# A neighbourhood-attention encoder layer: 23 key columns in the first block, values and gates requested earlier, raw attention-half weights split during attention

## The chip, the cores and the metric

The kernel runs on one core of one Trainium2 chip. Its time is the device time of one execution in microseconds, and the figure that is compared is the median of several executions. The profile is one more execution, recorded by the hardware profiler.

## The reference

One encoder layer is applied to a prompt (256 tokens, a grid of 4 rows) and to a sample (2048 tokens, 32 rows of 64 columns), all in float32. Half of the mixed width is neighbourhood attention, the other half a Fourier mixer.

```python
def neighbourhood_attention(q, k, v, rpb):          # window of 8 rows x 16 columns
    def one_row(r):
        rs = jnp.clip(r - kr // 2, 0, rows - kr)
        k_slab = lax.dynamic_slice_in_dim(kg, rs, kr, axis=1)[:, :, slab_cols]   # 32 columns per block of 16
        v_slab = lax.dynamic_slice_in_dim(vg, rs, kr, axis=1)[:, :, slab_cols]
        logits = jnp.einsum('bjqhd,bijkhd->bhjqik', q_blk, k_slab) * scale
        logits = jnp.where(valid[:, :, None, :], logits + bias, NEG_INF)
        p = softmax(logits)
        return jnp.einsum('bhjqik,bijkhd->bjqhd', p, v_slab)

def encoder_layer(x, ...):
    h = rms_norm(x, g_pre)
    q, k, v, z_a, u_f, z_f = jnp.split(h @ w_in, ...)          # six parts of 512
    y_a = neighbourhood_attention(q, k, v, rpb)                # 8 heads of 64
    y_f = fourier_mix(u_f, w_fourier, b_fourier)
    mixed = jnp.concatenate([rms_norm(y_a, g_na) * silu(z_a), rms_norm(y_f, g_f) * silu(z_f)], -1)
    return x + rms_norm(mixed @ w_out, g_post)
```

A query column of the first block (columns 0 to 15) sees key columns 0 to 22 at most, one of the last block (48 to 63) key columns 40 to 63.

## The kernel before

Each float32 product of the projections is three matmuls on a high and a low part (`mm3`). The program has four stretches: projections up to about 550 us, the Fourier mixer up to about 612, attention up to about 860, and the output's last product. The order of the instructions on each engine is the order of the code (`manual_schedule`); every DMA goes out on SP's queue except one or two at the start on ACT's, and each transfer waits on one of eight semaphores in turn, so for the landing of the one eight before it.

The projections use their own weights and, between them, prepare `w_out`: `wo_load` fetches a raw block of 128 x 1024, `wo_split` makes the high and low part on ACT and DVE (scaled by `gmix`) and stores both in `woD`. There are eight blocks: 0 to 3 belong to the attention half, 4 to 7 to the Fourier half.

Attention is 36 groups in four rounds, one round for each pair of heads (`pr`), nine groups in a round (`i`): the prompt, then row blocks `R` = 0 to 3 in two column halves `hc`. A group holds 256 queries in two blocks of columns (`b`); `KW` gives the key columns that are kept for the four blocks, 24, 32, 32, 24. A group of `R` > 0 has 11 key rows in reach, a group of `R` = 0 has 8. One step `k` of the loop works on two groups at once: for the new group `g` = G[k] the score matmuls (tile `s`), bias and minimum on DVE (`bias_max`), the exponentials on ACT (`exps`), the scaling on POOL (`soft`); for the group before it, `f` = G[k-1], the transposes of the weights (`transp`, tile `ptb`), their copies (`pt`) and the product with the values (`pv`). Between them PE does half a tile of the Fourier half's output product (`f_mm`, tile `po`), which `f_evac` scales and stores in `oD`. Its operands come by `ys_load`, `ys_mul` (gate `yz`, on POOL) and `ys_split`.

At the end of step `k`, `prep_v` requests the values and gate `za` of G[k+1] (three buffers, `VB`) and `prep` the queries of G[k+3]. The values lie in `vD`, one array of rows for each block of columns. With 24 columns, four key rows fill 96 partitions, and 11 rows make three chunks of 96, 96 and 72; `ch` lists the chunks that are transposed and `pp` the pv matmuls. `load_t` and `mask_p` bring and mask the bias tables of the next round: the table is requested in step i = 5 and masked in step i = 8. From step 24 to 31 the split weights of the attention half come back from `woD`, 512 KB a step.

After the last attention step come 18 tiles of output (`a_mm`, `evac`, `factor`, `residual`). `last_tile` is the last of them; it also finishes the tile before it, `b`.

Of the kernel before, what the change touches and what calls it, by code (L numbers as in the profile page):

```python
# [31 lines left out]
KW = (24, 32, 32, 24)  # L32
# [9 lines left out]
VB = 3  # L42
# [3 lines left out]
def constants():  # L46
# [62 lines left out]
    for p in range(128):  # L109
        half, i, qc = p // 64, p // 16 % 4, p % 16  # L110
        for b in range(2):
            cb = 2 * b + half
            ws = min(max(16 * cb + qc - 8, 0), 48)
            kc = KP0[cb] + np.arange(32)
            cm[p, b] = np.where((kc >= ws) & (kc < ws + 16), 0.0, BIG)
        for cb, j in ((0, slice(0, 24)), (1, slice(24, 56)), (3, slice(56, 80))):
# [62 lines left out]
def build(tc, A, O):  # L179
# [20 lines left out]
    woD = dr.tile([2, 2, 4, 128, D], F32, name="woD")  # L200
# [169 lines left out]
    VC = ((0, 0, 0, 24, 0), (1, 0, 8, 24, 0), (1, 1, 0, 8, 24), (2, 0, 24, 8, 0), (2, 1, 0, 24, 8), (3, 1, 8, 24, 0))  # L370
# [253 lines left out]
    def x_part(c, kp, q=nc.sync):  # L624
        if kp == 0:
            xs[c] = gt(BS, F32, "xr")
        ks = slice(2 * kp, 2 * kp + 2)
        q.dma_start(xs[c][:, ks], xsrc(c)[:, ks])
# [72 lines left out]
    def wo_load(x):  # L701
        wor[x] = load((128, D), A["wo"][x // 4, x % 4], "wr")

    def wo_split(x):
        w = wor.pop(x)
        g = gmix[:, x:x + 1]
        o = k8(F32R, "wo", (128, 2, D))
        nc.scalar.activation(o[:, 0], w, AF.Copy, scale=g)
        nc.vector.scalar_tensor_tensor(out=o[:, 1], in0=w, scalar=g, in1=f_(o[:, 0]), op0=ALU.mult, op1=ALU.subtract)
        for y in range(2):  # L710
            nc.sync.dma_start(woD[x // 4, y, x % 4], f_(o[:, y]))
# [118 lines left out]
    for i in range(16):  # L830
        sg, pr = divmod(i, 8)
        if i == 8:
            hooks.clear()
            for x in (5, 6):
                at(2 * x - 9, b_split, x)
            for x in range(8):
                if x:
                    at(3 * x - 2, wo_load, x)
                at(3 * x + 2, wo_split, x)
            at(20, w_load, 8)  # L840
            at(24, w_sums, 8)
            for j in range(7):
                at(24 + j // 2, a_split, 8, j)
            vu(1, range(4), hooks)
# [271 lines left out]
    def prep_v(g):  # L1116
# [99 lines left out]
    for n in range(2):  # L1216
        for c in range(4):
            nc.sync.dma_start(wo1[n][c].bitcast(F32),
                              woD[1, :, c, :, n * 512:n * 512 + 512].rearrange("x p d -> p x d"))
# [159 lines left out]
    def ys_load(d):  # L1379
# [141 lines left out]

    NT = {4: range(2, 4), 8: range(4, 8), 10: range(8, 13), 12: range(13, 18)}
# [19 lines left out]
    ys_load(ftiles[2])  # L1542
    prep_v(G[2])
    prep(G[4])
    for k in range(2, len(G) + 1):
# [11 lines left out]
        if k == 23:  # L1557
# [34 lines left out]
        if g:  # L1592
            soft(g, 1)
            if k == 2:
                ys_mul(ftiles[x])
                ys_load(ftiles[x + 1])
# [8 lines left out]
        if pr < 3 and i == 8:  # L1605
# [11 lines left out]
        if k + 1 < len(G):  # L1617
            prep_v(G[k + 1])
# [38 lines left out]

    def factor(d, q=1):
        sa, r = d["sa"], d["r"]
        s, y, x = r[:, 0:1], r[:, 1:2], r[:, 2:3]  # L1660
        V.tensor_scalar(s, sa[:, q:q + 1], -0.5 / D, sa[:, 4:5], ALU.mult, ALU.add)
# [3 lines left out]
    def residual(d, n):  # L1665
        of, xt, s = d["of"], d["xt"], d["r"][:, 0:1]
        ns = slice(n * 512, n * 512 + 512)
        if "og" in d:
            V.scalar_tensor_tensor(out=xt[:, ns], in0=d["og"][:, ns], scalar=s, in1=xt[:, ns], op0=ALU.mult,
                                   op1=ALU.add)  # L1670
        else:
            V.scalar_tensor_tensor(out=of[:, ns], in0=ptb[n], scalar=s, in1=of[:, ns], op0=ALU.mult, op1=ALU.mult)
            nc.gpsimd.tensor_tensor(out=xt[:, ns], in0=of[:, ns], in1=xt[:, ns], op=ALU.add)
# [3 lines left out]
    def last_tile(d, b):  # L1677
# [17 lines left out]
        V.tensor_tensor(out=og[:, 512:], in0=ptb[1], in1=d["of"][:, 512:], op=ALU.mult)  # L1695
        factor(d, 3)
        for n in range(2):
            residual(d, n)
# [49 lines left out]
```

## Time and profile before

| | |
|---|---|
| median of the runs | 959.66 us (958.94 to 960.04, 3 runs) |
| the profiled execution | 962.69 us |
| its span, first to last instruction | 960.9 us |
| PE, weight loads | 947.7, 792.8 us busy |
| DVE, ACT, POOL | 666.7, 468.3, 342.1 us busy |
| DMA | 270.64 MB, 282 GB/s in the mean |
| granted TensorE clock, mean | 0.996 |

In the rows of a profile, PE is the matmul engine and PEld its weight loads, DVE, ACT and POOL are the vector, scalar and general engines, SP issues DMAs. `L1484` is a line of the kernel, `pv<-pt,v` says that the instruction writes tile `pv` and reads `pt` and `v`, and `x32` counts instructions. A row of the timeline or of the chain starts with its start and its length in us. A row of the waits names who waited, for whom, for how long in total, how often, and the longest.

### The profile page before, as it was taken

The page shows a single profiled execution, that of the slowest core. Times are in us where ns is not written, and L with a number is a line of the kernel's source. Part 1 is how long each engine was busy: PE and PEld are TensorE (multiplying, and loading weights), DVE is VectorE, ACT ScalarE, POOL GpSimd, SP SyncE. Part 2 cuts the span into 40 slices and gives each one's busy share as a digit, 9 for nine tenths or more (in the row PEclk, how much of TensorE's full clock was granted, in tenths as well). Part 3 has the DMA queues.
Part 4 walks back from the last instruction along what each step waited for, and adds up shares of the span by engine and source line. Part 5 has one row for each costly group of instructions (what it writes and reads, how often), then busy time and mean ns, then how long its engine had stood idle before and what let it go on. Part 6 is the DMA issues. An engine that isn't in the chain of part 4 may idle for free.

```text
span 960.9 us, 17852 instructions
## 1 busy us (share of the span) xinstructions
PE 947.7 (99%) x6240; PEld 792.8 (83%) x6240; DVE 666.7 (69%) x1303; ACT 468.3 (49%) x1035; POOL 342.1 (36%) x338
## 2 busy tenths in 40 slices
PE   8999999999999999999999999999999998999996
PEld 7889988888888888888888888888887886888885
DVE  6387988676866976786667354676656655559997
ACT  6745676522332632233444144666555655544443
POOL 3101202445750401534433000554456555424444
PEclk9999999999999999999999999999999999999999
DMA  9899686458666999479989788599888899899993
GB/s 343 313 356 365 216 291 249 164 229 287 249 232 238 355 414 328 185 258 330 323 277 327 265 304 314 207 252 269 279 266 258 258 284 281 259 307 332 346 339 118
DMA packets 158361, 270.64 MB, mean 282 GB/s; under 512 B 22656, under 2 KB 98304, under 8 KB 155392
## 3 DMA queue, kind: packets, MB, share of 16 engines
q1 hardware_dynamic: 157984, 269.37, 81.4%
q8 instruction: 50, 0.82, 0.3%
q14 instruction: 39, 0.32, 0.1%
q10 hardware_dynamic: 288, 0.14, 0.1%
HBM read 180.91 MB, written 95.88 MB: 288 GB/s over the span
## 4 chain that ended last, share of the span: by engine, by line
PE 95%; DMA 2%; DVE 1%; issue 1%; SPq 0%; ACT 0%; DVEq 0%; ACTq 0%
PE po L1413 19%; PE mm L175 18%; PE mm L176 18%; PE mm L174 18%; PE pv L1484 5%; PE ptb L1467 4%; PE s L1169 4%; PE pab L1014 2%; DMA v<-vD 1%; PE py L174 1%; PE py L176 1%; PE py L175 1%; DMA q<-qD 1%; DMA xr<-xt 0%; PE ppq L1051 0%
## 5 line engine op out<-in xcount | busy, mean ns | idle before, releaser
L174 PE MATMUL mm<-xh,wa 128*128 128x512 f32 x448 | 174.4, 389 | 0.0
L175 PE MATMUL mm<-xl,wa 128*128 128x512 f32 x448 | 174.3, 389 | 0.0
L176 PE MATMUL mm<-xh,wa 128*128 128x512 f32 x448 | 174.3, 389 | 0.0
L1203 POOL TENSOR_SCALAR w<-w,m 128x352 f32<-128x352 f32 (+4 forms) x136 | 77.3, 583 | 61.8 <-DVE m L1200 54.0
L176 PEld LDWEIGHTS mm<-xh,wa 128*128 128x128 f32 x448 | 84.1, 188 | 17.6
L174 PEld LDWEIGHTS mm<-xh,wa 128*128 128x128 f32 x448 | 84.1, 188 | 17.4
L175 PEld LDWEIGHTS mm<-xl,wa 128*128 128x128 f32 x448 | 84.1, 188 | 17.4
L1413 PE MATMUL po<-wo,yh 128*128 128x512 f32 x272 | 90.4, 413 | 0.0
L551 POOL TENSOR_TENSOR ws<-wr 128x512 f32<-128x512 f32 x16 | 22.4, 1397 | 185.9 <-DMA wr<-wz 105.2
L1413 PE MATMUL po<-w,yh 128*128 128x512 f32 x280 | 86.7, 391 | 0.0
L566 DVE TENSOR_TENSOR wa<-wr,wa 128x512 fp32r<-128x512 f32 x60 | 55.0, 924 | 34.7 <-ACT wa L565 34.6
L1196 ACT ACTIVATE w<-w,m 128x352 f32<-128x352 f32 (+4 forms) x136 | 70.2, 519 | 13.3 <-DVE m L1191 13.1
L175 PE MATMUL mm<-vl,xh 128*128 128x512 f32 x168 | 65.5, 390 | 0.2 <-DVE vl L497 0.2
L174 PE MATMUL mm<-vh,xh 128*128 128x512 f32 x168 | 65.4, 389 | 0.0
L176 PE MATMUL mm<-vh,xl 128*128 128x512 f32 x168 | 65.4, 389 | 0.0
L868 DVE TENSOR_TENSOR f<-u,mm 128x512 f32<-128x512 f32 x64 | 43.5, 680 | 30.4 <-PE mm L176 25.8
L1413 PEld LDWEIGHTS po<-w,yh 128*128 128x128 f32 x280 | 52.3, 188 | 10.8
L1191 DVE CUSTOM_DVE_ANT_1 w<-s,tb 128x264 f32<-128x264 f32 (+3 forms) x124 | 51.6, 453 | 11.4 <-PE s L1169 10.9
L1484 PEld LDWEIGHTS pv<-pt,v 96*64 96x64 f32 (+2 forms) x1088 | 45.1, 137 | 15.1 <-issue 11.7
L565 ACT CAST wa<-wr 128x512 fp32r<-128x512 f32 x60 | 36.3, 618 | 41.6 <-PE mm L176 17.7
L1413 PE MATMUL po<-w,yl 128*128 128x512 f32 x140 | 54.5, 389 | 0.0
L1413 PE MATMUL po<-wo,yl 128*128 128x512 f32 x136 | 53.5, 393 | 0.0
(245 smaller groups left out, 2212.3 us busy)
## 6 DMA issues: line engine op xcount, KB each, us to landing
wr<-wz SPq DMA_DIRECT2D x48, 512.0 KB
vl<-sD SPq DMA_DIRECT2D x20, 512.0 KB
xm<-xm SPq DMA_DIRECT2D x9, 1024.0 KB
oD<-ofs SPq DMA_DIRECT2D x18, 512.0 KB
of<-oD SPq DMA_DIRECT2D x18, 512.0 KB
yr<-yD SPq DMA_DIRECT2D x34, 256.0 KB
zD<-f SPq DMA_DIRECT2D x16, 512.0 KB
woD<-wo SPq DMA_DIRECT2D x16, 512.0 KB
```

The costliest lines, as they stand in the source:

```text
L174: nc.tensor.matmul(out, lh, rh, start=first, stop=False)
L175: nc.tensor.matmul(out, lh, rl, start=False, stop=False)
L176: nc.tensor.matmul(out, ll, rh, start=False, stop=last)
L566: nc.vector.tensor_tensor(out=o[:, 1], in0=src, in1=o[:, 0].bitcast(F32), op=ALU.subtract)
L868: nc.vector.tensor_tensor(out=dst(f, b), in0=src(uu[u]), in1=src(p), op=op)
L1169: nc.tensor.matmul(sp[2 * b + h][64 * y:64 * y + 64, j * w:(j + n) * w], g["q"][hs, 128 * b + 64 * y:128 * b + 64 * y + 64], kk[hs, k:k + ...
L1191: nc.vector.tensor_tensor_reduce(out=rows(g["w"][b][:, h, :n], w), in0=rows(g["s"][2 * b + h][:, :n], w), in1=tv, scale=1.0, scalar=3.0e38 ...
L1196: nc.scalar.activation(w, w, AF.Exp, bias=m[:, h:h + 1], scale=-1.0, accum_out=m[:, 2 + h:3 + h])
L1203: nc.gpsimd.tensor_scalar(w, w, m[:, 4 + h:5 + h], 1.0, ALU.mult, ALU.mult)
L1413: nc.tensor.matmul(p, (d["l"] if x == 2 else d["h"])[:, c], w(n, int(x == 1), c), start=j == 0, stop=j == 11)
L1467: nc.tensor.transpose(ptb[h][:nk, j * 128:j * 128 + 128], g["w"][b][:, h, c0:c0 + nk], ident)
L1484: nc.tensor.matmul(p[hs, b, o], g["v"][:nk, v, hs], g["pt"][b][:nk, h, j * 128 + o.start:j * 128 + o.stop], start=first, stop=last)
```

## The change

The first block keeps 23 key columns. Eleven rows are then 253 keys, which make two chunks, of 128 and 125, cut without regard to rows; the values of such a group come in three requests (256 rows as two blocks of 128, then 92 and 36 rows), and its four partial-window products use a third block that holds the rows shared by both halves of queries in the order that the first chunk has. `VB` becomes 4, and values and gates are requested for G[k+2]; Fourier tiles and their gates one tile earlier, `yz` in two buffers. The table of the next round is masked in step i = 7. Only the Fourier half of `w_out` is split in the projections; the raw attention half is fetched in eight parts of 128 x 512 in every second step from 13 to 27 and split in the even steps from 18 to 32. At the start `x_part(0, 0)` goes out on SP's queue. In `last_tile` the rest of tile `b` and the half mean move, and the last sums are cut into two parts of 384 on DVE and one of 256 on ACT and POOL.

```diff
-KW = (24, 32, 32, 24)
+KW = (23, 32, 32, 24)
...
-VB = 3
+VB = 4
...
+    nc.scalar.dma_start(gpre, A["gpre"])
     nc.sync.dma_start(RV[0][:, 0], A["wv"][0][:, 0])
-    nc.scalar.dma_start(gpre, A["gpre"])
-    x_part(0, 0, nc.scalar)
+    x_part(0, 0)
...
-            for x in range(8):
+            for x in range(4):
                 if x:
-                    at(3 * x - 2, wo_load, x)
-                at(3 * x + 2, wo_split, x)
+                    at(6 * x - 2, wo_load, x)
+                at(6 * x + 2, wo_split, x)
...
+            if g["R"] and 11 * w <= 256:
+                vs = src.rearrange("r c e -> (r c) e")[:, cs]
+                k0, k1, m = (r0 - 4) * w, (r1 + 3) * w, 11 * w - 128
+                nc.sync.dma_start(v[:, 4 * b:4 * b + 2], vs[k0:k0 + 256].rearrange("(j p) e -> p j e", p=128))
+                nc.sync.dma_start(v[:n, 4 * b + 2], vs[k1:k1 + n])
+                nc.sync.dma_start(v[n:, 4 * b + 2], vs[k0 + n:k0 + 128])
+                g["ch"].append([(0, 128), (128, m)])
+                g["pp"].append([(1, None, m, 4 * b + 1, True, False), (0, 0, 128, 4 * b, False, False),
+                                (0, 1, 128, 4 * b + 2, False, True)])
+                continue
...
-            d["z"] = sm.tile([128, 4, 128], F32, tag="yz", name="yz", bufs=1)
+            d["z"] = sm.tile([128, 4, 128], F32, tag="yz", name="yz", bufs=2)
...
+    def wo_split_a(y):
+        c, ns = wo_part(y)
+        h, l, w = WO[0][:, c, ns], WO[1][:, c, ns], wraw[:, y % 4 * 512:y % 4 * 512 + 512]
+        nc.scalar.activation(h, w, AF.Copy, scale=gmix[:, c:c + 1])
+        V.scalar_tensor_tensor(out=l, in0=w, scalar=gmix[:, c:c + 1], in1=h.bitcast(F32), op0=ALU.mult,
+                               op1=ALU.subtract)
...
-        if 24 <= k < 32:
-            y = k - 24
-            nc.sync.dma_start(WO[y % 2][:, y // 2].bitcast(F32), woD[0, y % 2, y // 2])
+        if 13 <= k < 29 and k % 2:
+            y = (k - 13) // 2
+            c, ns = wo_part(y)
+            nc.sync.dma_start(wraw[:, y % 4 * 512:y % 4 * 512 + 512], A["wo"][0, c][:, ns])
...
-                if x + 1 < 18:
-                    ys_load(ftiles[x + 1])
+                if x + 2 < 18:
+                    ys_load(ftiles[x + 2])
...
+        if 18 <= k < 34 and k % 2 == 0:
+            wo_split_a((k - 18) // 2)
...
-        if pr < 3 and i == 8:
+        if pr < 3 and i == 7:
             mask_p(pr + 1)
...
-        if k + 1 < len(G):
-            prep_v(G[k + 1])
+        if k + 2 < len(G):
+            prep_v(G[k + 2])
...
-        residual(b, 1)
         sa = d["sa"]
         V.tensor_scalar(sa[:, 0:1], sa[:, 0:1], sa[:, 1:2], None, ALU.add)
         part_sum(sa)
+        residual(b, 1)
         guess(d, 3)
+        half_mean(d, 3)
         V.tensor_tensor(out=og[:, 512:], in0=ptb[1], in1=d["of"][:, 512:], op=ALU.mult)
         factor(d, 3)
-        for n in range(2):
-            residual(d, n)
+        xt, f = d["xt"], d["r"][:, 0:1]
+        nc.scalar.activation(og[:, 768:], og[:, 768:], AF.Copy, scale=f)
+        nc.gpsimd.tensor_tensor(out=xt[:, 768:], in0=og[:, 768:], in1=xt[:, 768:], op=ALU.add)
+        for q, ns in ((nc.sync, slice(0, 384)), (nc.sync, slice(384, 768)), (nc.scalar, slice(768, 1024))):
+            if ns.stop < D:
+                V.scalar_tensor_tensor(out=xt[:, ns], in0=og[:, ns], scalar=f, in1=xt[:, ns], op0=ALU.mult, op1=ALU.add)
+            q.dma_start(O["yo"][d["t"] * 128:d["t"] * 128 + 128, ns], xt[:, ns])
```

On PE, in the step in which the last group of column half 0 of round 0 is transposed and multiplied with its values, the kernel before has these rows (a row is line, operation, out<-in, shape, count; `ptb` is a transpose, `pv` a product with values):

```order
L1467 MATMUL ptb<-ident,w 96x128 x2
L1467 MATMUL ptb<-ident,w 72x128
L1467 MATMUL ptb<-ident,w 96x128 x2
L1467 MATMUL ptb<-ident,w 72x128
...
L1484 MATMUL pv<-pt,v 64x128 x4
L1484 MATMUL pv<-pt,v 64x64 x4
L1484 MATMUL pv<-pt,v 64x128 x4
L1484 MATMUL pv<-pt,v 64x64 x4
```

and the changed kernel these:

```order
L1477 MATMUL ptb<-ident,w 128x128
L1477 MATMUL ptb<-ident,w 125x128
L1477 MATMUL ptb<-ident,w 128x128
L1477 MATMUL ptb<-ident,w 125x128
...
L1494 MATMUL pv<-pt,v 64x128 x2
L1494 MATMUL pv<-pt,v 64x64 x4
L1494 MATMUL pv<-pt,v 64x128 x4
L1494 MATMUL pv<-pt,v 64x64 x4
```

Block 0 has four transposes for six and two wide products for four; block 1 is as it was.

On SP, around the turn to the last round (steps 26 to 28), the kernel before requests the values of the first group of the sample (`vD_64`, `vD_65`) behind the table `tb`, a block of split weights `w` and two stores:

```order
L1085 DMA tb<-tD 128x2x880
L1562 DMA w_7838<-woD 128x1024
L1443 DMA oD<-ofs 128x1024
L1518 DMA yD<-y 128x512
L1134 DMA v<-vD_64 96x2x128 x2
L1134 DMA v<-vD_65 128x2x128 x2
L1146 DMA za<-zD 128x128 x2
L1113 DMA q<-qD 128x2x128
L1562 DMA w_7837<-woD 128x1024
```

In the changed kernel the same values stand ahead of the table, and behind it come a raw part `wraw` and the values of the group after:

```order
L1144 DMA v<-vD_64 92x2x128 x2
L1144 DMA v<-vD_65 128x2x128 x2
L1156 DMA za<-zD 128x128 x2
L1113 DMA q<-qD 128x2x64 x2
L1085 DMA tb<-tD 128x2x880
L1586 DMA wraw<-wo 128x512
L1453 DMA oD<-ofs 128x1024
L1528 DMA yD<-y 128x512
L1144 DMA v<-vD_66 128x2x128 x2
L1144 DMA v<-vD_67 96x2x128 x2
```

The values are one step further up; the queries (`q`) keep their step.

On DVE, at the end of the program, from the last evacuation on, before:

```order
L1638 SCALAR_TENSOR_TENSOR of<-pl,inva,of 128x128
L1672 SCALAR_TENSOR_TENSOR of<-ptb,sr,of 128x512
L1692 TENSOR_SCALAR sa<-sa 128x1
L1649 TENSOR_SCALAR sa<-sa 128x1
L1650 TENSOR_SCALAR sa<-sa 128x1
L1695 TENSOR_TENSOR og<-ptb,of 128x512
L1661 TENSOR_SCALAR sr<-sa 128x1
L1662 TENSOR_SCALAR sr<-sr 128x1
L1663 TENSOR_SCALAR sr<-sr 128x1
L1669 SCALAR_TENSOR_TENSOR xt<-og,sr,xt 128x512 x2
```

and after:

```order
L1664 SCALAR_TENSOR_TENSOR of<-pl,inva,of 128x128
L1717 TENSOR_SCALAR sa<-sa 128x1
L1675 TENSOR_SCALAR sa<-sa 128x1
L1676 TENSOR_SCALAR sa<-sa 128x1
L1698 SCALAR_TENSOR_TENSOR of<-ptb,sr,of 128x512
L1685 TENSOR_SCALAR sr<-sa 128x1
L1722 TENSOR_TENSOR og<-ptb,of 128x512
L1692 TENSOR_SCALAR sr<-sr 128x1
L1693 TENSOR_SCALAR sr<-sr 128x1
L1729 SCALAR_TENSOR_TENSOR xt<-og,sr,xt 128x384 x2
```

The product of the other tile (`of<-ptb,sr,of`) has moved from ahead of the three sums to behind them, and the half mean (L1661, now L1685) from behind `og` to ahead of it.

More of the change, by code (lines that the diff above doesn't have):

```diff
@@ L115, in constants @@
             cm[p, b] = np.where((kc >= ws) & (kc < ws + 16), 0.0, BIG)
-        for cb, j in ((0, slice(0, 24)), (1, slice(24, 56)), (3, slice(56, 80))):
+        for cb, j in ((0, slice(0, 23)), (1, slice(24, 56)), (3, slice(56, 80))):
             ws = min(max(16 * cb + qc - 8, 0), 48)
@@ L199, in build @@
     yD = dr.tile([2, 4, 128, T], F32, name="yD")
-    woD = dr.tile([2, 2, 4, 128, D], F32, name="woD")
+    woD = dr.tile([2, 4, 128, D], F32, name="woD")
     tD = dr.tile([4, 128, 2, 1520], F32, name="tD")
@@ L701, in wo_load @@
     def wo_load(x):
-        wor[x] = load((128, D), A["wo"][x // 4, x % 4], "wr")
+        wor[x] = load((128, D), A["wo"][1, x], "wr")
     def wo_split(x):
         w = wor.pop(x)
-        g = gmix[:, x:x + 1]
+        g = gmix[:, 4 + x:5 + x]
         o = k8(F32R, "wo", (128, 2, D))
@@ L710, in wo_split @@
         for y in range(2):
-            nc.sync.dma_start(woD[x // 4, y, x % 4], f_(o[:, y]))
+            nc.sync.dma_start(woD[y, x], f_(o[:, y]))
     wor = {}
@@ L1218, in build @@
             nc.sync.dma_start(wo1[n][c].bitcast(F32),
-                              woD[1, :, c, :, n * 512:n * 512 + 512].rearrange("x p d -> p x d"))
+                              woD[:, c, :, n * 512:n * 512 + 512].rearrange("x p d -> p x d"))
     prep(G[2])
@@ L1542, in build @@
     ys_load(ftiles[2])
+    ys_load(ftiles[3])
     prep_v(G[2])
     prep(G[4])
+    prep_v(G[3])
     for k in range(2, len(G) + 1):
@@ L1667, in residual @@
         ns = slice(n * 512, n * 512 + 512)
[L1668 to L1673, printed above, removed]
+        V.scalar_tensor_tensor(out=of[:, ns], in0=ptb[n], scalar=s, in1=of[:, ns], op0=ALU.mult, op1=ALU.mult)
+        nc.gpsimd.tensor_tensor(out=xt[:, ns], in0=of[:, ns], in1=xt[:, ns], op=ALU.add)
         nc.sync.dma_start(O["yo"][d["t"] * 128:d["t"] * 128 + 128, ns], xt[:, ns])
```

20 lines of the change are left out of this document (13 added, 7 removed).

## The prediction

> **What bounds the kernel now.** I read the page's first lines, then the tensor engine's waits, the busy time in stretches of 20 us, and last the chain of waits and the timeline at the places where the tensor engine (PE) stands still.
>
> ```profile
> span 960.9 us, 17852 instructions
> PE 947.7 (99%) x6240; PEld 792.8 (83%) x6240; DVE 666.7 (69%) x1303; ACT 468.3 (49%) x1035; POOL 342.1 (36%) x338
> ...
> PE pv L1484 <- DMA v<-vD: 1.9, 2, 1.7
> PE mm L174 <- DVE xh L295: 1.3, 1, 1.3
> PE s L1169 <- DMA q<-qD: 1.2, 3, 0.5
> ...
> 0.00:20.00 20.00, 17.58 (x69) 14.36 (x70) 12.19 (x25) 12.18 (x27) 5.36 (x9) 0.91 0.90 330
> 480.00:500.00 20.00, 20.00 (x90) 16.57 (x89) 13.92 (x18) 9.00 (x15) 7.90 (x6) 1.00 0.76 265
> 700.00:720.00 20.00, 20.00 (x228) 16.41 (x226) 12.41 (x42) 11.42 (x35) 11.28 (x17) 1.00 0.86 256
> 800.00:820.00 20.00, 16.97 (x208) 13.46 (x210) 9.52 (x32) 9.66 (x29) 9.12 (x16) 1.00 0.91 263
> 940.00:960.00 20.00, 13.49 (x69) 11.63 (x67) 15.09 (x36) 6.64 (x21) 8.94 (x7) 0.91 0.32 118
> ```
>
> Behind the length of each stretch stand PE, PEld, DVE, ACT and POOL busy, then PE's granted clock, the DMA engines' share and GB/s. PE idles 13.2 us in all: 2.4 in the first stretch, 3.0 at 800 to 820, 7.4 at the end, some 0.3 elsewhere. So time comes from fewer PE instructions, or from those three places; what is taken off another engine at 480 or 700 is worth nothing by itself.
>
> **The narrower keys.** Only the groups of column block 0 in row blocks R = 1 to 3 lose PE work: 3 in each of 4 head pairs, 12 in all. Each loses two of its twelve transposes and two of its sixteen pv matmuls, those 128 wide. The price is read from the length of an attention step, from the first score matmul to the next:
>
> ```profile
> 744.62 1.21 PE s L1169 x20
> 749.63 1.08 PE pv L1484 x32
> 750.71 1.21 PE s L1169 x20
> 756.14 1.50 PE pv L1484 x32
> 757.64 1.21 PE s L1169 x20
> 758.85 0.81 PE ptb L1467 x6
> ```
>
> A step takes 750.71 - 744.62 = 6.09 us when the group before had 8 transposes and 32 pv records 64 wide (two records to a matmul), and 757.64 - 750.71 = 6.93 with 12 transposes and half the records 128 wide. Of the 0.84 between, pv is 1.50 - 1.08 = 0.42; the other 0.42 is four transposes, 0.105 each. A narrow record is 1.08 / 32 = 0.034, a wide one (1.50 - 16 x 0.034) / 16 = 0.060. So a group loses 2 x 0.105 + 4 x 0.060 = 0.45 us; scores fall by 22 of 1232 columns of 1.21 us, 0.02. Twelve groups give 5.6, the four of R = 0 (184 columns for 192) 0.1 more: **-5.7 us**. Ends: 4.2 (wide records priced as narrow ones), 6.7 (0.81 / 6 a transpose). All of it is on PE's path, as no engine is near 20 of 20 at 700 to 720; DVE, ACT and POOL lose a little with it.
>
> **v and gates earlier, and no split weights fetched.** The last round (pr = 3) stalls:
>
> ```profile
> 733.94 0.92 PE s L1169 x16
> 771.49 1.21 PE s L1169 x20
> 791.67 0.92 PE s L1169 x16
> 794.23 8.58 DMA v<-vD
> 804.87 5.58 DMA v<-vD
> 814.21 5.09 DMA q<-qD
> 822.95 1.23 PE pna L1457 x12
> 835.15 1.21 PE s L1169 x20
> ...
> woD<-wo SPq DMA_DIRECT2D x16, 512.0 KB
> ...
> w<-woD SPq DMA_DIRECT2D x8, 512.0 KB
> tb<-tD SPq DMA_DIRECT2D x4, 880.0 KB
> ```
>
> From step 19 to step 25 round 2 takes 771.49 - 733.94 = 37.55 us; the same steps of round 3, 28 to 34, take 835.15 - 791.67 = 43.48, less 1.23 of pna matmuls that only they have, 42.25. So the stall is 4.7 us, of which the waits show 3.0; the rest hides in score matmuls that run slowly. Its cause stands beside it: v of step 28's group is issued on SP at 794.23, 2.6 after its step began, and lands 8.6 later, behind an 880 KB table, 512 KB of split weights and the store of oD. Round 2 moves 256 GB/s at a share of 0.86, so some 298 fill the engines; 512 KB in each step of about 6.5 us is 81 more, 337, too much.
>
> After the change v goes out a step earlier (6.9 us, where 2.6 of lateness made the first stall), ahead of that table, and the weights are eight loads of 256 KB in every second step from 13 to 27, half the bytes, none from step 28 on. q is not requested earlier; its 1.2 us of waits go only because SP is less late. I take all **-4.7** for the profiled execution; the lower end is 1 (q's waits stay and v gains little).
>
> The third request per group: SP issues 12 more transfers, some 0.45 us each by the issue at 1.17 below, on a queue that in round 2 makes PE wait nowhere. Cover: the step that v now has in hand; uncovered 12 x 0.45 = 5.4 us. The gates' second buffer and the tile loaded two ahead keep SP's wait for the POOL product of the same tile: 0, hidden the same way; v, za and oD queue behind that wait as before. Table masking one step sooner: one POOL instruction, three times, behind a load two steps old; POOL has 7.5 of 20 free. 0; a late table would hold up POOL's scaling and then the transposes, and only then cost.
>
> **The split in attention.** Eight times a 128x512 ACT scaling and a DVE subtraction, at the even steps 18 to 32, after both transposes' copies:
>
> ```profile
> 8.78 0.72 ACT L264 ACTIVATE wc<-rv,gpre 128x512 fp32r<-128x512 f32 x1
> 9.62 0.75 DVE L265 SCALAR_TENSOR_TENSOR wc<-rv,gpre,wc 128x512 fp32r<-128x512 f32 x1
> ```
>
> 0.75 us in every second step, where DVE idles 7.6 of 20 and ACT 8.6: 0. Behind it on DVE stand f_evac and pv's product, whose banks PE needs a step later. Uncovered: 8 x 0.75 = 6 us. What leaves the projections (four splits, eight stores) leaves a stretch with PE at 20.00 of 20: 0.
>
> **The start.** x's first part moves from ACT's queue to SP's, behind the first 256 KB of wv.
>
> ```profile
> 1.17 0.45 ACTq L628 DMA_DIRECT2D xr<-xt  x1
> 4.73 1.49 ACT L264 ACTIVATE wc<-rv,gpre 128x512 fp32r<-128x512 f32 x2 [1.59 <-DMA gpre<-gpre]
> 5.69 0.29 DVE L295 CAST xh<-xr 128x256 fp32r<-128x256 f32 x1 [4.79 <-DMA xr<-xt]
> 6.13 0.47 PE L174 MATMUL mm<-wc,xh 128*128 128x512 f32 x1 [1.33 <-DVE xh L295]
> ```
>
> PE's first product waits for x alone; its other operand is there at 4.73 + 0.75 = 5.48. An earlier x gains at most about 0.5; SP's later loads go out one issue, 0.45, later, so the loss is at most that. **-0.2**, since x no longer shares the engines with what SP queued after it.
>
> **The tail.** After the last matmul the chain runs on ACT and DVE.
>
> ```profile
> 952.40 0.61 DVE L1638 SCALAR_TENSOR_TENSOR of<-pl,inva,of 128x384 f32<-128x384 f32 x1
> 953.79 0.74 DVE L1672 SCALAR_TENSOR_TENSOR of<-ptb,sr,of 128x512 f32<-128x512 f32 x1
> 954.88 0.15 DVE L1650 TENSOR_SCALAR sa<-sa 128x1 f32<-128x1 f32 x1
> 954.95 0.68 DVE L1695 TENSOR_TENSOR og<-ptb,of 128x512 f32<-128x512 f32 x1
> 955.54 0.21 DVE L1661 TENSOR_SCALAR sr<-sa 128x1 f32<-128x1 f32 x1
> 956.17 0.21 DVE L1663 TENSOR_SCALAR sr<-sr 128x1 f32<-128x1 f32 x1
> 956.47 1.42 DVE L1669 SCALAR_TENSOR_TENSOR xt<-og,sr,xt 128x512 f32<-128x512 f32 x2
> ```
>
> The other tile's 0.74 at 953.79 was free, inside ACT's squares; now it stands ahead of og: +0.74. The half mean moves ahead of og and leaves the chain: -0.3. The last adds are two of 0.61 in place of two of 0.71, with 256 columns on ACT and POOL beside them: -0.2; the last transfer is smaller: -0.05. **+0.2**, ends -0.3 and +0.7.
>
> **Sum.** The profiled execution took 962.69 (span 960.9 and 1.8 around it): 962.69 - 5.7 - 4.7 - 0.2 + 0.2 = 952.3. The median of the runs is 959.66, 3.0 less, and since PE's busy time is the same work, that must come out of its idle places. If all of it is stall that the timed runs don't have, only 4.7 - 3.0 = 1.7 is left to win there: 959.66 - 5.7 - 1.7 = 952.3. If none, 959.66 - 10.4 = 949.3. No row says which, so I take the middle, **950.8**.
>
> **Rivals.** (a) The stall stays: SP remains late through the extra issues, q is as late as before, and only PE's work falls: 959.66 - 5.7 = 954.0, up to 956.5 if 2.5 of new stall comes with it. For it: q's waits. Against it: 3.5 MB less in the last round (2 x 256 KB for 8 x 512). (b) Slower: the DMA queue becomes the bound in rounds 1 and 2 as well, since the transfers of 92 and 36 rows and the raw weights come on top of a share of 0.86. Two more rounds with the stall of the last, 4.7 each, while the last keeps its own: 959.66 - 5.7 + 9.4 = 963.4. It decides from the point where a step's added transfer time passes 0.14 x 6.7 = 0.9 us; the raw weights are 256 KB in 13.4 us, 20 GB/s or 0.07, so the narrow transfers would have to bring another 0.07, and eat the step that v has gained. (c) The split holds up PE: 950.8 + 6 = 956.8 with no cover at all; DVE's free 7.6 of 20 speaks against it.
>
> The Trainium skill (DMA: Bandwidth & Descriptors, "Why a DMA increments its semaphore by 16 and not by 1") speaks against this change: a transfer runs on the largest number of engines up to 16 that divides its outer dimension. By it 96 rows use 16 engines, but 92 only 4 and 36 twelve. Estimated by that page, the four engines get 18 more rows of 512 bytes for a group of R > 0 and 68 for R = 0, at 27 ns a row (298 GB/s over 16) 3.4 us in a round of 58, which with the raw weights stays just under the idle 0.14; by it (a) and (b) grow and the sum would go to some 954. No row of this trace has such a transfer.
>
> **How the numbers follow.** The forecast, with the stall gone for the most part (947.5 to 953): 0.62; (a) 953 to 957: 0.22; (b) 0.07; (c) and smaller mishaps of its kind, 956 to 959: 0.06; better than 947.5: 0.03. The range 947.5 to 956.5 leaves out (b), most of (c), and the last. About 0.2% is what this measurement can tell from no change, 957.7 to 961.6: faster 0.87 (the forecast, (a), better), same 0.06 (c), slower 0.07 (b).
>
> **What would show it.** Right: pv of the twelve groups at about 1.26 us and their first transposes x4; PE busy near 942; no PE wait on v or q after 780, 820 to 840 at 20.00; first product near 5.9; some 7.6 us behind the last matmul. Wrong: waits on v or q in steps 13 to 30 with the DMA share above 0.95, PE waiting on pt or w copies at even steps, or matmuls that take longer with 125 and 128 rows.

## The result, and the profile after

The changed kernel took 965.63 us in the median (962.40 to 968.11, 6 runs), the kernel before 959.66 (958.94 to 960.43, 6 runs on the same chip): a ratio of 1.0062, interval 1.0043 to 1.0081. It is slower by 6 us (0.6%), where 950.8 was forecast, and outside the range (947.5 to 956.5). The profiled execution took 968.11, the longest of the six, and its span is 966.3; the one before took 962.69.

The page's first lines, the tensor engine's waits, and the busy time in stretches (PE, PEld, DVE, ACT, POOL, then granted clock, DMA share, GB/s), after:

```profile
span 966.3 us, 17710 instructions
PE 944.9 (98%) x6168; PEld 788.5 (82%) x6168; DVE 669.8 (69%) x1307; ACT 469.6 (49%) x1040; POOL 349.2 (36%) x339
...
PE s L1179 <- DMA q<-qD: 11.9, 8, 2.9
...
700.00:720.00 20.00, 19.03 (x197) 15.04 (x190) 11.29 (x41) 11.19 (x35) 11.00 (x17) 1.00 0.84 253
720.00:740.00 20.00, 18.04 (x208) 14.69 (x204) 11.26 (x43) 10.92 (x37) 10.14 (x17) 1.00 0.87 266
780.00:800.00 20.00, 17.11 (x204) 13.91 (x203) 10.39 (x41) 10.44 (x33) 11.24 (x16) 1.00 0.87 249
800.00:820.00 20.00, 17.08 (x174) 13.16 (x176) 9.97 (x35) 9.46 (x31) 10.14 (x17) 0.83 0.89 264
```

The kernel before had, in two of the same stretches:

```profile
720.00:740.00 20.00, 20.00 (x237) 15.97 (x233) 11.79 (x47) 11.73 (x38) 10.94 (x18) 1.00 0.85 252
780.00:800.00 20.00, 20.00 (x206) 15.95 (x205) 12.05 (x52) 12.18 (x45) 12.51 (x21) 1.00 0.97 303
```

PE has 72 matmuls fewer, and the waits for v are gone. In their place stands one row: the score matmuls wait for q, eight times, 11.9 us, where it was 1.2. The stretches at 700, 720 and 780, in which PE was busy for 20 of 20 us before, now have 1 to 3 us of idle time each. The one at 800 keeps its 3 us and now also runs at a granted clock of 0.83. Why q is late stands in the chain of waits (start, length, what; pieces of 0.14 us and less left out), here at the step in which PE stands still for 2.9 us:

```profile
773.65 8.10 DMA oD<-ofs
781.77 2.68 DMA q<-qD
784.59 1.28 PE s L1179 x20
...
799.68 6.92 DMA oD<-ofs
806.62 4.32 DMA q<-qD
```

and in SP's rows of the timeline (start, length of the issue), with what SP waited for from 779 to 782 under them:

```profile
772.93 0.60 SPq L1586 DMA_DIRECT2D wraw<-wo  x1
773.65 0.35 SPq L1453 DMA_DIRECT2D oD<-ofs  x1
774.11 0.38 SPq L1528 DMA_DIRECT2D yD<-y  x1
774.58 0.88 SPq L1135 DMA_DIRECT2D v<-vD  x1
775.51 1.81 SPq L1136 DMA_DIRECT2D v<-vD  x1
777.37 0.50 SPq L1137 DMA_DIRECT2D v<-vD  x1
777.92 1.38 SPq L1144 DMA_DIRECT2D v<-vD  x2
779.62 0.33 SPq L1156 DMA_DIRECT2D za<-zD  x1
781.77 0.37 SPq L1113 DMA_DIRECT2D q<-qD  x1
...
SPq L1113 <- DMA oD<-ofs: 1.8, 1, 1.8
```

Count from the 512 KB store of `oD`: it, `yD`, three narrow requests, two of the other block, `za` are eight. q is the one after these, so it needs the semaphore of the store, which lands 8.10 us after its issue. SP has nothing to do from 779.95 to 781.77, the DMA engines are not full (0.87 in the mean of 780 to 800), and PE waits. With two requests instead of three q would have stood one place further forward, and would have waited for the landing of the request before the store instead. With eight requests in flight at most, eight go out in the landing time of a slow one, and a step of 6.5 us holds nine to ten (SP issues 58 from 650 to 690).

This block is 1.82 of the 2.90 us for which PE waits. In the second stall SP stands still for 0.91 us before the q at 806.62, of 2.92. The rest is that q comes last behind requests that are issued one after the other, each for 0.33 to 1.81 us in the rows above. In the second stall no third request stands between the store and q: `yD`, four requests of `v` and two of `za` do. So the third request is not alone in making q late.

What SP waited for in round 1 (668 to 728) shows how the queue has filled. The first rows for before, then after (who waited, for whom, total, times, longest):

```profile
SPq L1443 <- ACT ofs L1442: 3.8, 2, 2.1
SPq L1518 <- DVE y L1504: 2.2, 2, 1.3
```

```profile
SPq L1156 <- DMA yr<-yD: 1.0, 2, 0.5
SPq L1113 <- DMA oD<-ofs: 0.8, 1, 0.8
SPq L1528 <- DVE m L1210: 0.8, 2, 0.4
```

Before, SP waited for engines to finish what it was to store: it was abreast of them. After, no wait for an engine is above 0.8: SP is mostly behind, and a request's place in its queue then decides when it goes out.

The stall also costs clock. The last rows of the chain are another q behind another store; for it PE is idle from 808.16 to 811.08. In finer stretches, the first of them behind the 2.9 us at 781.69:

```profile
785.00:788.00 3.00, 3.00 (x35) 2.45 (x28) 2.18 (x10) 1.84 (x7) 0.00 (x0) 1.00 1.13 295
...
808.00:810.00 2.00, 0.16 (x6) 0.02 (x2) 0.42 (x1) 0.39 (x1) 0.15 (x1) 1.00 0.44 103
810.00:811.00 1.00, 0.00 (x0) 0.00 (x0) 0.00 (x0) 0.00 (x0) 1.00 (x2) 0.52 0.87 252
...
812.00:814.00 2.00, 2.00 (x19) 1.35 (x12) 1.23 (x6) 0.60 (x2) 0.00 (x0) 0.50 0.84 245
...
816.00:818.00 2.00, 2.00 (x11) 1.54 (x10) 0.49 (x2) 0.81 (x4) 0.51 (x2) 0.78 0.95 296
```

After this idle time PE works at half clock from 811 to about 817, which is some 3 us more: this stall counts twice. While PE stands still from 808 to 810, the DMA engines are busy for a share of 0.44 only.

### The profile page after: what moved, and what is told of

Same layout as the page of the kernel before. It is cut to its first block, busy times and chain, and to the rows that moved or that the text cites. A ratio compares the mean times of both kernels' runs of the same rounds, so it can differ in the third digit from the quotient of the medians.

```text
span 966.3 us, 17710 instructions
## 1 busy us (share of the span) xinstructions
PE 944.9 (98%) x6168; PEld 788.5 (82%) x6168; DVE 669.8 (69%) x1307; ACT 469.6 (49%) x1040; POOL 349.2 (36%) x339
## 4 chain that ended last, share of the span: by engine, by line
PE 87%; DMA 8%; SPq 2%; DVE 1%; issue 1%; POOL 0%; ACT 0%; POOLq 0%; DVEq 0%; ACTq 0%
PE mm L175 18%; PE mm L176 18%; PE mm L174 18%; PE po L1423 16%; DMA oD<-ofs 3%; PE ptb L1477 3%; PE s L1179 3%; PE pv L1494 3%; PE pab L1014 2%; DMA q<-qD 2%; DMA yz<-zD 1%; DMA v<-vD 1%; PE py L174 1%; PE py L176 1%; PE py L175 1%
## 5 line engine op out<-in xcount | busy, mean ns | idle before, releaser
L1213 POOL TENSOR_SCALAR w<-w,m 128x352 f32<-128x352 f32 (+6 forms) x136 | 81.5, 613 | 79.1 <-DVE m L1210 65.5
L1206 ACT ACTIVATE w<-w,m 128x352 f32<-128x352 f32 (+6 forms) x136 | 70.3, 521 | 25.9 <-DVE m L1201 25.8
L566 DVE TENSOR_TENSOR wa<-wr,wa 128x512 fp32r<-128x512 f32 x60 | 57.8, 972 | 33.6 <-ACT wa L565 33.6
L1201 DVE CUSTOM_DVE_ANT_1 w<-s,tb 128x352 f32<-128x352 f32 (+5 forms) x124 | 51.4, 452 | 24.7 <-PE s L1179 23.1
L1179 PE MATMUL s<-kk,q 64*64 64x128 f32 (+5 forms) x752 | 43.9, 346 | 12.0 <-DMA q<-qD 11.9
```

Source lines behind the costliest of these rows:

```text
L566: nc.vector.tensor_tensor(out=o[:, 1], in0=src, in1=o[:, 0].bitcast(F32), op=ALU.subtract)
L1179: nc.tensor.matmul(sp[2 * b + h][64 * y:64 * y + 64, j * w:(j + n) * w], g["q"][hs, 128 * b + 64 * y:128 * b + 64 * y + 64], kk[hs, k:k + ...
L1201: nc.vector.tensor_tensor_reduce(out=rows(g["w"][b][:, h, :n], w), in0=rows(g["s"][2 * b + h][:, :n], w), in1=tv, scale=1.0, scalar=3.0e38 ...
L1206: nc.scalar.activation(w, w, AF.Exp, bias=m[:, h:h + 1], scale=-1.0, accum_out=m[:, 2 + h:3 + h])
L1213: nc.gpsimd.tensor_scalar(w, w, m[:, 4 + h:5 + h], 1.0, ALU.mult, ALU.mult)
```

## The experiments

All ratios are to the kernel before in the same job, with a 95% interval. "Waits" are PE's in the one profiled execution of each run, which need not lie at its median: that of e1 took 967.69 us, that of e8 956.21.

| run | what | median us | ratio (interval) | waits us |
|---|---|---|---|---|
| after | | 965.63 | 1.0062 (1.0043-1.0081) | q 11.9 |
| e1 | after, 24 columns | 963.01 | 1.0038 (1.0020-1.0055) | q 5.3 |
| e2 | after, split weights as before | 965.30 | 1.0057 (1.0036-1.0078) | q 11.1 |
| e3 | after, v one ahead | 964.36 | 1.0041 (1.0023-1.0059) | v 4.7, q 3.1 |
| e4 | after, q four ahead | 962.22 | 1.0034 (1.0010-1.0058) | transposes 8.1 |
| e5 | after, 24 columns, three requests | 964.56 | 1.0056 (1.0033-1.0079) | q 4.8 |
| e6 | after, q ahead of v in the step | 963.38 | 1.0041 (1.0028-1.0055) | q 6.9 |
| e7 | after, q on ACT's queue | 983.86 | 1.0265 (1.0213-1.0318) | transposes 12.6 |
| e8 | before, 23 columns | 961.63 | 1.0031 (1.0012-1.0050) | q 1.7, v 2.5 |
| e9 | after, 64 and 64 rows | 968.16 | 1.0076 (1.0059-1.0093) | q 12.5 |
| e10 | after, one request of 128 rows | 960.66 | 1.0003 (0.9989-1.0016) | q 4.3 |
| e11 | before, start and last tile | 959.36 | 0.9989 (0.9978-1.0000) | q 0.7 |
| e12 | before, v two ahead | 965.31 | 1.0048 (1.0031-1.0065) | q 6.4 |
| e13 | after, za in one request | 959.55 | 0.9996 (0.9979-1.0013) | q 4.2 |
| e14 | after, yr and yz on POOL's queue | 996.48 | 1.0361 (1.0321-1.0401) | transposes 31.1 |
| e15 | e13, e14 and e6 together | 996.43 | 1.0369 (1.0330-1.0408) | transposes 30.6 |
| e16 | e8 and e11, fewer requests | 956.05 | 0.9965 (0.9950-0.9981) | v 0.8, q 0.4 |
| e17 | after, fewer requests, q ahead of v | 954.29 | 0.9944 (0.9930-0.9959) | q 2.3 |
| e18 | e17, 24 columns | 956.74 | 0.9969 (0.9956-0.9983) | none over 0.6 |

**Undo one part of the change.** First, which part brings the waits?

```diff
e1: -KW = (23, 32, 32, 24)
    +KW = (24, 32, 32, 24)
```

> The changed kernel with 24 key columns in the first block again, so that its values come in two requests of 96 rows; all else as changed. The changed kernel's profile has about 17 us of stall in attention, all of it before score matmuls that wait for q; without it it would take about 951. Theory N (the three narrow requests of 128, 92 and 36 rows slow SP's queue): the stall falls to 4 us or less, the PE work of 5.7 us comes back, 957 to 960. Theory W (the raw weights overload rounds 2 and 3): the stall stays near 14, 968 to 971. Theory V (v's earlier request takes the queue ahead of q): the same, 968 to 971.

```diff
e2: -            wo_split_a((k - 18) // 2)
    +            nc.sync.dma_start(WO[y % 2][:, y // 2].bitcast(F32), woD[0, y % 2, y // 2])   # k = 24 to 31
```

> The changed kernel with the attention half of the weights split in the projections and fetched as 512 KB a step from 24 to 31, as before the change. Theory W: the stalls of rounds 2 and 3 (steps 14 to 26, some 8 us) go, those of round 1 stay, and the last round stalls by 5 or more: 958 to 964. Theories N and V: rounds 1 to 3 as in the changed kernel, the last round worse by some 3 us: 966 to 972.

```diff
e3: -VB = 4
    +VB = 3
    -            prep_v(G[k + 2])
    +            prep_v(G[k + 1])
```

> The changed kernel with three value buffers and values requested one step ahead, as before the change; 23 columns and raw weights stay. Theory V: q waits vanish, little stall is left, 951 to 955. Theory N: the lateness of the queue stays, q waits as in the changed kernel and v waits beside them, 966 to 975. Theory W: rounds 2 and 3 stall as changed, round 1 is clean, 962 to 968.

```diff
e4: -            prep(G[k + 3])
    +            prep(G[k + 4])      # and q in five buffers
```

> The changed kernel with the queries requested four steps ahead in five buffers, so that q has one step (6.5 to 6.9 us) more in hand. If the queue is late by a bounded 5 us or so (any of N, V, W as the cause), the waits for q go and none takes their place: 950 to 954. If the queue's rate itself is below what the steps ask for, lateness grows until something else waits: 960 or more.

No single part brings the time back. With 24 columns PE has 5 us more to do, and the kernel is still no slower than with 23: the narrow requests cost at least what the narrow keys save. The weights (e2) make no difference to the time. The gains of e3 and e4 are not resolved, as their intervals overlap that of the changed kernel. With v one ahead both v and q are late. With q four ahead nothing waits for q, but other rows come up:

```profile
PE ptb L1477 <- POOL ysq L1521: 4.9, 1, 4.9
PE ptb L1477 <- ACT pt L1479: 3.2, 1, 3.2
```

POOL is in its squares and gate products, whose operands come through the same queue. So the waits move between q, v and, as far as these rows show it, the Fourier tiles, according to who stands last in the queue.

**Shape, number, or place?**

```diff
e5: e1, and
    +  parts = ((0, 2, r0 - 4), (2, 1, r0 + 4), (3, 1, r1 + 3))   # first block's 12 groups: 192, 96, 96 rows
```

> The changed kernel with 24 columns, where the values of the first block's twelve groups are fetched by three requests of 96 rows each in place of two (192... rows in one, 96 in the other): the count of requests of the changed kernel without its 92- and 36-row shapes. Theory S (SP's in-order queue is full, each request in it makes q later): 3 us slower than the kernel with 24 columns and two requests (963.0), so 966 to 969, with 7 to 12 us of waits for q. Theory N (the shape of the narrow requests costs, not their number): 962 to 964, waits for q as there, about 5.

```diff
e6: -            prep_v(G[k + 2])
    -            prep(G[k + 3])
    +            prep(G[k + 3])
    +            prep_v(G[k + 2])
```

> The changed kernel with the last two calls of a step exchanged: q of the group three ahead is requested before the values of the group two ahead. The same requests, bytes and shapes. Theory S (place in SP's queue decides): q moves up by some four requests, about 2.5 us, and its waits fall from 11.9 us to under 4; 957 to 961. Theory N or B (the narrow shapes, or the bytes, keep the DMA engines busy too long): no change within 2 us, 964 to 967.

```diff
e7: in prep
    -            nc.sync.dma_start(ql..., q)
    +            nc.scalar.dma_start(ql..., q)
```

> The changed kernel with q's requests on ACT's queue instead of SP's; same bytes and shapes. Theory S: no PE wait for q, SP loses 43 requests (21 us of issuing in four rounds) and the time falls to 951 to 957; ACT pays some 0.5 us a request, 20 us in all, beside 50% idle time. Theory B (the DMA engines are full): q lands as late as before or something else (the Fourier tiles, v) lands late instead, 962 to 967.

```diff
e8: the kernel before, with
    -KW = (24, 32, 32, 24)
    +KW = (23, 32, 32, 24)      # and the three requests of prep_v
```

> The kernel before with 23 columns alone (the new shapes of values, transposes and products; everything else as before). Theory S (a full queue needs both the earlier v and the extra requests): PE's work falls by 5 us, SP in round 1 has 6.9 us of spare time to take 3 more requests; 955 to 958. Theory N (narrow requests alone make the stall): v or q waits of 7 us or more, 961 to 965.

In e5 the two requests of 24 columns, 288 and 96 rows, become three of 192, 96 and 96 (not 96 each, as its expectation has it). Its interval overlaps that of e1, so the third request is not resolved there. e6 gains 2 us, less than the place alone promised, and its interval overlaps that of the changed kernel; PE still waits 6.9 us for q. e7 takes q out of SP's order, but puts ACT behind the same landings. PE's waits row, and ACT's timeline at one of these places:

```profile
PE ptb L1477 <- ACT pt L1479: 12.6, 10, 3.4
...
684.74 1.31 ACTq L1113 DMA_DIRECT2D q<-qD  x2
686.10 0.59 ACT L1206 ACTIVATE w<-w,m 128x352 f32<-128x352 f32 x1 [5.40 <-DMA v<-vD]
```

ACT stands idle for 5.40 us, most of it before its two requests of q, and its copies of the transposes queue behind them; the time is 20 us worse, and the theory of a queue that one merely has to leave got no support from it. e8 is the clearest: with nothing else changed, the narrow keys lose 3 us where PE saves 5. Its profiled execution took 956.21 with a mean granted clock of 0.998, another run 964.29 with 0.992; 0.006 x 960 = 5.8 us is an estimate of the most that the clock, the second price of a stall, can make of these 8.

```diff
e9: -                nc.sync.dma_start(v[:n, 4 * b + 2], vs[k1:k1 + n])
    -                nc.sync.dma_start(v[n:, 4 * b + 2], vs[k0 + n:k0 + 128])
    +                nc.sync.dma_start(v[:64, 4 * b + 2], vs[k1:k1 + 64])
    +                nc.sync.dma_start(v[64:, 4 * b + 2], vs[k0 + 64:k0 + 128])
e10:+                nc.sync.dma_start(v[:, 4 * b + 2], vs[k0:k0 + 128])     # in place of both
```

> The changed kernel with the third block of a narrow group fetched as 64 and 64 rows in place of 92 and 36: three requests and the same bytes, but 28 keys of the block are other rows than the product needs, so only time is read here. Theory N (the shape: by the Trainium skill, DMA: Bandwidth & Descriptors, 92 rows go to few engines and make these late): the waits for q shrink from 11.9 us to some 4, 957 to 961. Theory C (the number of requests and the place in the queue): like the changed kernel, 964 to 967, 8 to 13 us of waits for q.

> As the run with 64 and 64 rows, but the third block in one request of 128 rows, so two requests per narrow group as with 24 columns (the second half's keys are other rows than needed; time alone is read). Theory N: as with 64 and 64, 957 to 961. Theory C: 2 to 4 us less than the changed kernel, 961 to 963. If neither shape nor number matters (the earlier v and the raw weights alone make the stall): 964 to 967.

The waits row of e9, then of e10:

```profile
PE s L1179 <- DMA q<-qD: 12.5, 8, 3.3
```

```profile
PE s L1178 <- DMA q<-qD: 4.3, 4, 1.9
```

The same bytes in three requests of other shapes: no gain. The same bytes in two requests: 0.0059 of 960, 5.7 us, for 12 requests fewer, and the intervals lie apart. The Trainium skill (DMA: Bandwidth & Descriptors, "Why a DMA increments its semaphore by 16 and not by 1") lets a transfer of 92 rows run on four engines and one of 64 on sixteen; whether it did so no run shows, but if it did, it cost nothing that e9 could give back. Of shape and number, the number is what counts.

**Two parts alone.**

```diff
e11: the kernel before with the changed first requests and the changed last_tile
e12: the kernel before, with
    -VB = 3
    +VB = 4
    -            prep_v(G[k + 1])
    +            prep_v(G[k + 2])
```

> The kernel before with the changed start and the changed last tile alone. By the profiles of before and after, the first product comes 1.2 us earlier and the end 0.07 earlier: 957.8 to 959, no change in attention's waits beyond their scatter. If the earlier start only moves a wait behind it: 959 to 960.

> The kernel before with values and gates requested two groups ahead (four buffers) alone. My forecast's step: the last round's stall goes, 955 to 957, no wait for v or q. Theory S (v far too early pushes q back in SP's queue): v's waits go, q's waits rise to 3 to 6 us, 960 to 964.

The ends give 1.1 us (0 to 2.1 by the interval), as the profiles said. v two groups ahead, the step that was to bring 4.7 us, costs 4.6 by itself. The chain of e12 at its longest stall (again without the pieces of 0.14 us and less):

```profile
794.69 7.74 DMA oD<-ofs
802.44 4.57 DMA q<-qD
807.15 2.33 PE s L1169 x20
```

It is the same store, in the same last round where before had waited for v: the wait has changed its name, and in one piece of 4.5 us (clock 0.50 behind it) it costs more than in small ones. Steps 28 to 34 take 46.12 us there, where they took 43.48 before.

**Take requests away.**

```diff
e13: in prep_v
    -            nc.sync.dma_start(g["za"][:, x:x + n], zD[1, cs, t0:t0 + n])     # for each half
    +        nc.sync.dma_start(g["za"].rearrange("p (n x) -> p n x", x=128), z[:, n0:n1 + 1:n1 - n0])
e14: in ys_load
    -        nc.sync.dma_start(d["raw"], ...)
    +        nc.gpsimd.dma_start(d["raw"], ...)        # and d["z"]
e15: e13, e14 and e6
```

> The changed kernel with the gate za of a group in one request, also where its two halves lie apart (16 groups: 16 requests fewer on SP's queue, the same bytes in the same pieces). Theory C (the number of requests in SP's queue): by the 12 requests that were worth 5.0 us between the changed kernel and the run with one block of 128 rows, 0.4 us each, 16 are worth up to 6.7: 959 to 962, with waits for q of 3 to 6 us. Theory B (the bytes on the DMA engines): no change, 964 to 967.

> The changed kernel with the loads of the Fourier tiles and their gates (yr, yz: 34 requests in attention) on POOL's queue instead of SP's; the same bytes. Theory C: SP is free of 9 requests a round, its waits for other engines come back (5 us and more in round 1), no wait for q over 1 us, 951 to 956. Theory B: q or the tiles land as late as before, 963 to 967. If POOL pays for issuing (its products hold up the transposes): waits of the transposes for POOL or ACT, 960 to 966.

> Both, and q requested ahead of v in a step. Theory C: the forecast's time, 950 to 954, no wait of PE for q. Theory B: 961 to 967.

e13 moves the same bytes in 16 requests fewer and is 0.0066, 6.3 us, faster than the changed kernel: 0.4 us each, as e10 had priced them. Bytes are not what was short. e14 (which moves 32 loads, not the 34 of its expectation) and e15 say nothing on SP's queue: POOL pays, and everything behind it, by 30 us more than even the expectation's worst case.

```profile
PE ptb L1478 <- POOL w L1213: 31.1, 14, 9.3
```

**Fewer requests still.** Now the gated Fourier tiles too: `yD` and `zD` become planes of one DRAM tensor, so that a tile and its gate come in one request (16 fewer again).

```diff
e16, e17:
    -        nc.sync.dma_start(d["raw"], yD[half, :, :, ts].rearrange("c p t -> p c t"))
    -            nc.sync.dma_start(d["z"], zD[0, :, ts].rearrange("(c p) t -> p c t", p=128))
    +            nc.sync.dma_start(b, zy[0:2, :, ts].rearrange("k (c p) t -> p (k c) t", p=128))
```

> The kernel before with 23 columns and the changed start and last tile, and with fewer requests: za of a group in one (16 fewer), a Fourier tile and its gate in one (16 fewer; both arrays lie in one DRAM tensor), values one group ahead as before. Attention has 20 requests fewer than before, 32 fewer than the kernel before with 23 columns (961.6). Theory C (number of requests in SP's queue): the stall goes, 959.7 - 5.5 (PE) - 0.8 (ends) - 3 (stall) = 950 to 952, waits for v and q under 2 us. Theory B (bytes): 957 to 960, as that kernel with its ends.

> The changed kernel with both merged requests (32 fewer in attention) and q requested ahead of v in a step. Theory C: 965.6 - 6.1 (merged gates, as measured) - 16 x 0.4 (merged tiles), as far as there is stall left, so 951 to 954, waits for q under 1.5 us. Theory B: 957 to 960, like the run with merged gates alone (959.55).

> The run with merged requests, q first and v two ahead (954.3, 0.9944 of before) with 24 columns: PE's work rises by 5.5 us, SP has 12 requests fewer. Theory C with room in the queue: the narrower keys are now worth what PE saves, so 958 to 960. If their 12 requests still cost as much as PE saves (0.4 us each, 4.8): 954 to 956.

PE's busy time and its waits row in e17:

```profile
PE 942.3 (99%) x6168; PEld 787.3 (83%) x6168; DVE 665.6 (70%) x1307; ACT 468.2 (49%) x1040; POOL 345.6 (36%) x339
...
PE s L1179 <- DMA q<-qD: 2.3, 3, 1.8
```

e17 beats both kernels: 0.0118 below the changed one, 11 us for 32 requests and q's place, and 5.4 below before. e16 fell short of its 950 to 952: it keeps v one ahead and 512 KB a step of split weights in the last round, where steps 28 to 34 take 39.89 us (38.03 in e17), and its clock is lower (0.994 to 0.999, e17 0.997 to 0.998). Which of these makes the difference was not tried. e18 took the middle between its two expectations: with room in the queue the narrow keys are worth 0.0025, 2.4 of the 5 us that PE saves; the intervals just overlap.

With fewer requests the last round also does what was forecast for it. The first scores of steps 28 and 34 in e18, which has the 24 columns of the kernel before:

```profile
791.18 0.99 PE L1179 MATMUL s<-kk,q 64*64 64x192 f32 x16
...
829.99 1.28 PE L1179 MATMUL s<-kk,q 64*64 64x264 f32 x24
```

That is 38.81 us, less the prediction's 1.23 of pna matmuls 37.58, where the prediction reads 42.25 for this stretch before and 37.55 for the same steps of round 2: the whole stall of 4.7 us is gone.

## Why the prediction was wrong, point by point

**The narrower keys: right on PE.** PE's rows at a step that follows a narrow group, as in the prediction's 6.93:

```profile
753.52 1.28 PE L1179 MATMUL s<-kk,q 64*64 64x352 f32 x24
...
758.75 1.35 PE L1494 MATMUL pv<-pt,v 125*64 125x128 f32 x28
760.02 1.26 PE L1179 MATMUL s<-kk,q 64*64 64x253 f32 x24
```

760.02 - 753.52 = 6.50, a cut of 0.43 for 0.45; twelve of them 5.2. (The ends given for this term, 4.2 and 6.7, come to 4.5 and 6.5 by its own figures; nothing hangs on that.)

**The third request: a step that failed.** I set it at 0, "Cover: the step that v now has in hand; uncovered 12 x 0.45 = 5.4". The uncovered price was right (5.7 in e10); the cover was the wrong one. v's slack covers only what v itself loses. The request stands in one queue with q, and q had no step in hand: with one more (e4) PE's waits for q vanish. I looked at who waits for the moved transfer, and not at who stands behind it. The 0.45 was read from a row of ACT's queue at the start, before anything queued; SP's issues of the three narrow requests take 0.38 to 0.65 us in the median and up to 2.1.

**v and gates earlier: the other step that failed, wrong in sign.** -4.7 was forecast, together with the split weights; v and the gates alone measured +4.6 (e12). That v would not be waited for was right. That q's waits "go only because SP is less late" was not: SP was no less late, since the requests were as many, and v's earlier place was paid for by those behind it. The 4.7 us were there to be won, as e18 shows, but only after requests had been taken out of the queue. "Ahead of that table" was the reasoning, and the store of `oD` and q were not in it.

**The split weights and the split in attention: 0 in the sum (e2), but not in each round.** In the profiled execution of e2, which fetches 512 KB of split weights a step again, the first scores of steps 28 and 34 are these:

```profile
792.15 0.97 PE L1179 MATMUL s<-kk,q 64*64 64x184 f32 x16
...
838.37 1.26 PE L1179 MATMUL s<-kk,q 64*64 64x253 f32 x24
```

That is 46.22 us, against 43.60 in the changed kernel (797.42 to 841.02): leaving out the split weights does help the last round, by 2.6. But from step 9 to step 28, where the eight raw parts are now fetched, the changed kernel takes 129.8 us and e2 124.5. By the medians the loads cost at one place what they gain at the other. This compares one execution with one, and the changed kernel's is its slowest.

**The start: right in sign, too small.** The first scaling, the first cast of x, the first product, and the first scores of attention, after:

```profile
4.18 0.72 ACT L264 ACTIVATE wc<-rv,gpre 128x512 fp32r<-128x512 f32 x1 [1.53 <-DMA gpre<-gpre]
4.50 0.29 DVE L295 CAST xh<-xr 128x256 fp32r<-128x256 f32 x1 [3.60 <-DMA xr<-xt]
4.96 0.50 PE L174 MATMUL mm<-wc,xh 128*128 128x512 f32 x1
...
604.58 0.32 PE L1179 MATMUL s<-kk,q 64*64 64x128 f32 x1
```

The product came 1.17 earlier (6.13 before), where I allowed 0.5, and the first scores 1.58 (606.16 before). My bound was the other operand, held fixed at 5.48; but its scaling waits for `gpre` in both kernels, and that too started earlier, by 4.73 - 4.18 = 0.55.

**The tail: +0.2 forecast, about -0.1 measured**, within its ends. Both ends alone give 1.1 us (e11).

**The sum.** Profiled execution against profiled execution: -5.2 keys, -1.6 up to the first scores, -0.1 tail, and 968.11 - 962.69 + 6.9 = 12.3 of new stall, of which some 3 are the half clock after 808. By the first score matmuls of the rounds, the new stall is 2.8, 3.5, 5.0 and 1.4 us in rounds 0 to 3 (how much longer each takes, plus the 1.3 us that PE saves in each). Rival (b) had nearly the outcome, 963.4 for 965.63, at a chance of 0.07, and the rounds nearly right: 4.7 each in rounds 1 and 2. Its cause was not the one. It put the stall down to transfer time on full DMA engines, but the share was 0.84 to 0.89 in the four stretches above with 1 to 3 us of idle time, not above 0.95, and the same bytes in fewer requests were faster (e10, e13). I had the eight semaphores in the description of the kernel and left them out of the sum.

What stays open is why each request costs what it does. Issue times (1.81 for the 92 rows above, though 0.41 in the median of the twelve; 0.35 for the store) and landing times (8.10) both lengthen the queue, and no run parts them. From 690 to 730 SP issues 56 requests, whose rows add up to 34.2 of the 40 us, so its issuing alone may be the limit as well as the eight semaphores. A queue with more in flight wasn't tried.

## What to carry to other kernels

Before moving a transfer earlier, count the requests in its in-order queue per step and name what it overtakes: where the queue is full, slack is only handed from one tile to another. A request added there has its price even if its own data are early, and merging two requests gives that back. The price was 0.4 to 0.5 us in the cleanest pairs (e10 and e13 against the changed kernel). In others it came out at 0.1 (e5 against e1, not resolved), 0.2 (e17 against e18) and 0.7 (e8), so it seems to depend on how full the queue is. A stall of 2 to 3 us on the tensor engine can cost up to 3.4 us more in granted clock, or nothing more.

## What the runs showed of the hardware

The clock fell after 2.92 us of idle PE (808.16 to 811.08, granted 0.52 from 810 on), but not after 2.90 at 781.69, where 785 on shows 1.00. In other runs it fell with shorter gaps, and stayed with some longer ones. PE's row behind the gap in e17, and the clock after it:

```profile
659.45 1.49 PE L1179 MATMUL s<-kk,q 64*64 64x352 f32 x24 [1.79 <-DMA q<-qD]
...
661.00:662.00 1.00, 1.00 (x5) 1.00 (x6) 0.78 (x4) 0.98 (x4) 0.00 (x0) 0.50 0.99 285
```

Here the clock fell at 660.3, when PE was already working again. It also fell with gaps of 1.76 (e6), 1.90 (e10) and 2.22 us (e13), and not with 2.48 (e5). So the length of a gap alone does not decide. In each of these falls the clock stayed down for 3.41 us (e6, e10, e17) or 6.83 us (e13 and the changed kernel), which at 0.50 costs up to 1.7 or 3.4 us. The Trainium skill (TensorE: Matmul & The Clock Gate, "Part 1: The HAM clock gate (the "warmup" mystery)") puts the fall after an idle window of about 3.4 us whose phase runs free. The free phase agrees with one gap of two being followed by a fall, and 3.41 and 6.83 us are one and two times the window. A whole idle window is not needed, since none of 3.4 us fits into 2.92 or 1.79, and the measurement decides. Requests moved to the queue of an engine that computes were not free: on ACT's they held up its copies (12.6 us of PE's waits in e7), on POOL's its scaling (31.1 in e14).
